# Splitting the down projection's first operand and weights under the second half of the last up product, with the halves of that product swapped

## The chip, the core and the metric

The kernel runs on one NeuronCore of a Trainium2 chip. The metric is the device time of one execution in microseconds. Three executions of the kernel before took 1459.34, 1459.81 and 1460.95 us; the median is 1459.81.

## What is computed

One inference step of a decoder layer with 1024 prompt tokens and 64 sample tokens (8 sequences of 8), width 1024, inner width 2816, all in 32-bit floats. The layer has a mixing part (stick-breaking attention and a convolution branch) and a channel part; the change touches only the channel part:

```
h2 = x * (1 + sc2) + sh2
val, gt = split(h2 @ w_up)                 # w_up: 1024 x 5632
gt_c = causal_dwconv(gt, width 3)          # per channel, along the tokens
f = (gelu(gt_c) * val) @ w_down            # w_down: 2816 x 1024
x = layernorm(alpha * x + (1 + g2) * f)
```

## The kernel before, in words

**Numbers.** Every matmul operand is split into a high and a low part of TensorE's 32-bit format: `split` (lines 594 to 596) makes the high part with a copy on ScalarE and the low part with a subtraction on VectorE. A product is then three matmuls: high by high, high by low, low by high.

**The up projection.** The 2816 inner channels are 22 feature tiles of 128. For each, `up_weights(f)` loads two 512 KB rows of `w_up` into two buffers of the ring `raw` (three buffers of 4 KB per partition) and makes seven 512-wide combinations of them, split into `W[0]` to `W[6]`. `up(f, ...)` multiplies them with the seven prepared combinations of the tokens: a fast matrix multiplication with seven half-size products in place of eight. The tokens come in two groups g of 272 columns for each product: `X[0]` lies in the pool `h2x`, `X[1]` (called Y in the profile, allocated at line 1571) in the six slots of ring "kv" in pool `kvp` and the two slots of ring "wo" in pool `wop`. A group's seven products of 12 matmuls go into three PSUM banks, and after each product `evacuate` (lines 1728 to 1742) reads its bank: products 0 and 3 on ScalarE, the others on VectorE. Product 3 may start when product 0 has been read, 4 after 1, 5 after 2 and 6 after 4. Feature tiles 1 to 20 take both groups together; the last one, 21, takes group 0 (X) and then group 1 (Y), line 1842.

**The gate.** `gate(f)` (lines 1812 to 1834) runs the width-3 convolution on VectorE (lines 1824 to 1828), gelu on ScalarE (1829) and the multiplication with the values on GpSimd (1831), and stores the result to DRAM scratch `fscr` and `fsscr` from SP's queue (1832, 1833).

**The down projection.** Three groups of feature tiles (8, 7 and 7) are accumulated over nine token tiles. For each token tile `f_tile` loads the gated features (line 1919) and splits them into `ft`; `prefetch` loads rows of `w_down` (line 626, called from 1908), 512 KB each, through `raw`, and splits them into a ring of 12 buffers `wd` of 8 KB. A token tile of the first group takes 8 x 6 = 48 matmuls of 512 columns (line 1942) into a pair of PSUM banks, which is copied to `acc` (line 1957). The weights of all later feature tiles reuse the 12 slots in turn.

**Where buffers lie.** The pools on the left side of the memory are stacked: `kvp`, `wop`, `arn` (with `W[4]`, `W[5]` and a sum), `h2x`, `gpp`. They are closed after the last gate (line 1848) and the pool `wdp` of the down projection (ring "ft" of two slots, "wd" of twelve, "fr" of two) is opened over the same bytes, so `ft` and the first weights lie where Y was. The first feature load is the exception: it goes to a `raw` buffer (line 1917). A wait is set for each buffer and each earlier reader of its bytes.

**What sets the order.** The stages up to the first up product are ordered by a planner inside the kernel. From there on (lines 1836 and following) the order of instructions on each engine and on SP's DMA queue is set at build time by the framework, which simulates the program's time line and lets instructions of the same engine pass each other where the data allows; on the chip every engine then keeps that fixed order.

Of the kernel before, what the change touches and what calls it, by code (L numbers as in the profile page):

```python
# [7 lines left out]
F32 = mybir.dt.float32  # L8
F32R = mybir.dt.float32r
# [7 lines left out]
D = 1024  # L17
TP = 1024
TS = 64
T = TP + TS  # L20
KT = 8
NFF = 22
# [10 lines left out]
NW = 12  # L33
KVB = 6
# [28 lines left out]
GROUPS = ((0, 8), (8, 15), (15, NFF))  # L63
# [409 lines left out]
def body(nc, tc, d):  # L473
    V, A, G, PE, SY = nc.vector, nc.scalar, nc.gpsimd, nc.tensor, nc.sync
# [14 lines left out]
    per = Open(name="per")  # L489
    rawp = Open(name="rawp")  # L490
    drp = Open(name="drp", space=DRAM)
    catp = Open(name="catp", side="right")
# [7 lines left out]
    def raw(shape, dt=F32):  # L500
        return rawp.tile(shape, dt, "raw", bufs=3)
# [7 lines left out]
    def vc(n, i=0, j=None, k=1):  # L509
        a = VEC[n][0] + i  # L510
        return vec[:, a:a + (k if j is None else j - i)]
# [19 lines left out]
    fscr = drp.tile([128, 4, NFF, 256], F32, "fscr")  # L531
    fsscr = drp.tile([128, NFF, TS], F32, "fsscr")
# [61 lines left out]
    def split(x, hi, lo):  # L594
        A.activation(hi, x, AF.Copy)  # L595
        V.tensor_sub(lo, x, hi)  # L596
# [22 lines left out]
        split(r, h, l)  # L619
        return h, l  # L620

    def split_pair(src, pool, name, bufs, r=None):

        if r is None:
            r = raw([128, D])
        SY.dma_start(r, src)
        w = pool.tile([128, 2, D], F32R, name, bufs=bufs)
        split(r, w[:, 0], w[:, 1])
        return w

# [312 lines left out]
    psS = Open(name="psS", space=PSUM)  # L943
    scr = [psS.tile([128, 2, 256], F32, f"scr{i}") for i in range(2)]
    psB = Open(name="psB", space=PSUM)
    kvp = Open(name="kvp")
# [296 lines left out]
    wop = []  # L1243
# [159 lines left out]
    wop, arn = wop  # L1403
# [4 lines left out]
    h2x = Open(name="h2x")  # L1408
    gpp = Open(name="gpp")
    vtp = Open(name="vtp", side="right")  # L1410
    cp = Open(name="cp", side="right")
    psC = Open(name="psC", space=PSUM)
# [4 lines left out]
    def bank():  # L1417
        npu[0] += 1
        return pus[(npu[0] - 1) % 8]
# [373 lines left out]
    dp = Open(name="dp", side="right")  # L1793
# [5 lines left out]
    def up(f, gss, vt, gp, gs):  # L1799
        for gg in gss:  # L1800
            P = [{g: bank() for g in gg} for _ in range(3)]
            for i in range(7):
                p = P[SUMS[i]]
                for kt in range(4):
                    for wt, xt, n in ((0, 0, 0), (0, 1, 1), (1, 0, 2)):
                        for g in gg:
                            PE.matmul(p[g][:, 0:NB], W[i][wt][:, 128 * kt:128 * kt + 128], X[g][kt][xt][:, i, :],  # L1807
                                      start=i < 3 and kt == 0 and n == 0, stop=kt == 3 and n == 2, skip_group_check=True)
                for g in gg:
                    evacuate(i, p[g], g, vt, gp, gs)  # L1810

    def gate(f, vt, gp, gs):
        V.memset(gp[:, 0:2], 0.0)
        V.tensor_copy(gs[:, :, 0:2], sft[:, f])
        V.tensor_copy(fop[:, f], gp[:, TP:TP + 2])
        V.tensor_copy(fos[:, f], gs[:, :, 8:10])
        c = dp.tile([128, 4, NB], F32, "gc", bufs=2)
        cp_, cs_ = c[:, :, 0:256], c[:, :, 256:NB].rearrange("p a (b t) -> p a b t", t=8)
        for k in range(3):
            w = vc("w_fdw", f * 3 + k)  # L1820
            gpk = gp[:, k:k + TP].rearrange("p (a i) -> p a i", a=4)
            gsk = gs[:, :, k:k + 8].rearrange("p (a b) t -> p a b t", a=4)
            if k == 0:
                V.tensor_scalar(cp_, gpk, w, vc("b_fdw", f), op0=OP.mult, op1=OP.add)
                V.tensor_scalar(cs_, gsk, w, vc("b_fdw", f), op0=OP.mult, op1=OP.add)
            else:
                V.scalar_tensor_tensor(cp_, gpk, w, cp_, op0=OP.mult, op1=OP.add)
                V.scalar_tensor_tensor(cs_, gsk, w, cs_, op0=OP.mult, op1=OP.add)
        gelu = A.activation(c, c, AF.Gelu).ins
        v4 = vt.rearrange("p h g i -> p (h g) i")  # L1830
        G.tensor_tensor(v4, v4, c, op=OP.mult)
        SY.dma_start(fscr[:, :, f, :], v4[:, :, 0:256])
        SY.dma_start(fsscr[:, f].rearrange("p (a i) -> p a i", a=4), v4[:, :, 256:NB])
        return gelu

    gate(0, vtb(), gp0(), gs0)
    for f in range(1, NFF):
        if f > 1:
            up_weights(f)
        t = (dp.tile([128, 2, 2, NB], F32, "vt", bufs=2), dp.tile([128, 2 + TP], F32, "gp", bufs=2),  # L1840
             dp.tile([128, 8, 10], F32, "gs", bufs=2))
        up(f, ((0,), (1,)) if f == NFF - 1 else ((0, 1),), *t)
        gelu = gate(f, *t)
    G.dma_start(d["ffn_p"], fop)
    G.dma_start(d["ffn_s"], fos)
    with tc.issue_after(gelu):
        pre[0] = A.preload_act_table_set(NLE).ins
    for p in (gpp, h2x, arn, wop, kvp, psC, psS, dp, vtp, catp):
        p.close()


    wdp = Open(name="wdp")
    ep = Open(name="ep", side="right")
    psE = Open(name="psE", space=PSUM)
    acc = [ep.tile([128, D], F32, f"acc{i}") for i in range(9)]
# [2 lines left out]
    def load_rows(i):  # L1858
        rows[i] = ep.tile([128, 2, D], F32, "rows", bufs=1)
        SY.dma_start(rows[i], d["lnr"][2 * i:2 * i + 2].unsqueeze(0).to_broadcast([128, 2, D]))  # L1860
        if i == 0:
            A.activation(rows[0], rows[0], AF.Copy, scale=ALPHA)
# [38 lines left out]
            V.scalar_tensor_tensor(y[0:n, h], y[0:n, h], r, rows[1][0:n, 1, h], op0=OP.mult, op1=OP.add)  # L1901
            SY.dma_start(d["y"][t0:t0 + n, h], y[0:n, h])

    ws = []

    def prefetch(n):
        for f in range(len(ws), min(n, NFF)):
            ws.append(split_pair(d["w_down"][f], wdp, "wd", NW))

    def f_tile(grp, tt):  # L1910
        f0, f1 = GROUPS[grp]
        nf, n = f1 - f0, min(128, T - 128 * tt)
        if grp or tt:
            fr = wdp.tile([128, 8, 128], F32, "fr", bufs=2)[:, 0:nf, 0:n]
        else:

            fr = raw([128, 1024]).rearrange("p (f n) -> p f n", n=128)
        fx = wdp.tile([128, 2, 8, 128], F32R, "ft", bufs=2)
        SY.dma_start(fr, fscr[:, tt // 2, f0:f1, 128 * (tt % 2):128 * (tt % 2) + n] if tt < 8 else fsscr[:, f0:f1])
        if tt < 8:  # L1920
            split(fr, fx[:, 0, 0:nf], fx[:, 1, 0:nf])
            return fx, ((0, 0), (0, 1), (1, 0))
        split(fr, fx[:, 0, 0:nf, 0:TS], fx[:, 0, 0:nf, TS:128])
        return fx, ((0, 0), (0, 1))

    for grp, (f0, f1) in enumerate(GROUPS):
        nf = f1 - f0
        for tt in range(9) if grp < 2 else (8, *range(8)):
            t0 = 128 * tt
            n = min(128, T - t0)  # L1930
            fx, passes = f_tile(grp, tt)
            prefetch(f1)
            last = (grp, tt) == (2, 7)
            pd = [psE.tile([128, 2, 512], F32, "pd", bufs=4) for _ in range(4 if last else 1)]
            pd = [p[:, 0, 0:256] for p in pd] if last else [pd[0][:, c] for c in range(2)]
            cw = D // len(pd)
            for cs_ in [(c,) for c in range(4)] if last else [(0, 1)]:
                for i in range(nf):
                    w = ws[f0 + i]
                    for xt, wt in passes:  # L1940
                        for c in cs_:
                            PE.matmul(pd[c], fx[:, xt, i], w[:, wt, cw * c:cw * c + cw],  # L1942
                                      start=i == 0 and (xt, wt) == passes[0], stop=i == nf - 1 and (xt, wt) == passes[-1])
            prefetch(min(len(ws) + 1, f0 + NW))
            if (grp, tt) == (0, 2):
                load_rows(0)
                load_gates()
            if (grp, tt) == (1, 8):
                load_rows(1)
            a, g = acc[tt], g2.get("p" if tt < 8 else "s")  # L1950
            if grp == 2:
                finish(tt, pd, t0, n, g)
                continue
            for c in range(2):
                h = slice(512 * c, 512 * c + 512)
                if grp == 0:
                    V.tensor_copy(a[:, h], pd[c])
                else:
                    V.tensor_add(a[:, h], a[:, h], pd[c])
            if grp == 1:  # L1960
                x = ep.tile([128, D], F32, "fx", bufs=2)
                SY.dma_start(x[0:n], xscr[t0:t0 + n, :])
                G.tensor_tensor(x[0:n], x[0:n], rows[0][0:n, 0], op=OP.mult)  # L1963
                G.tensor_tensor(x[0:n], x[0:n], rows[0][0:n, 1], op=OP.add)
                V.tensor_mul(a, a, g)
                V.tensor_add(a[0:n], a[0:n], x[0:n])
    for p in (psE, ep, wdp, drp, rawp, per):
        p.close()


# [80 lines left out]
```

## Time and profile before

| | us |
|---|---|
| median of the three runs | 1459.81 |
| the profiled execution | 1459.86 |
| its span, from the first to the last instruction | 1458.1 |
| TensorE (matmuls) busy | 1406.1 |
| VectorE busy | 1069.2 |
| ScalarE busy | 618.4 |
| GpSimd busy | 579.8 |

Read it as a chain that runs almost wholly on TensorE; the mean granted clock of TensorE over the span is 0.984 of 2.4 GHz. Positions in the text are microseconds from the start of the span. The last feature tile's up product runs from about 1160 to 1182, the down projection from there to about 1449. In the profile PE is TensorE, PEld its weight loads, DVE VectorE, ACT ScalarE, POOL GpSimd, SPq SP's queue of DMA issues. In a line of a timeline the bracket gives the engine's idle time just before it and what ended it; several like instructions are merged into one line with their count.

### The profile page before, as it was taken

The page shows a single profiled execution, that of the slowest core. Times are in us where ns is not written, and L with a number is a line of the kernel's source. Part 1 is how long each engine was busy: PE and PEld are TensorE (multiplying, and loading weights), DVE is VectorE, ACT ScalarE, POOL GpSimd, SP SyncE. Part 2 cuts the span into 40 slices and gives each one's busy share as a digit, 9 for nine tenths or more (in the row PEclk, how much of TensorE's full clock was granted, in tenths as well). Part 3 has the DMA queues.
Part 4 walks back from the last instruction along what each step waited for, and adds up shares of the span by engine and source line. Part 5 has one row for each costly group of instructions (what it writes and reads, how often), then busy time and mean ns, then how long its engine had stood idle before and what let it go on. Part 6 is the DMA issues. An engine that isn't in the chain of part 4 may idle for free.

```text
span 1458.1 us, 26948 instructions
## 1 busy us (share of the span) xinstructions
PE 1406.1 (96%) x10254; PEld 1224.0 (84%) x10254; DVE 1069.2 (73%) x1903; ACT 618.4 (42%) x1236; POOL 579.8 (40%) x433
## 2 busy tenths in 40 slices
PE   7999999998999999799899999999999989999997
PEld 4898899985666666588799999999999978888886
DVE  4799997536677666587978877787777754168798
ACT  2454524638888888233543332333333332031110
POOL 0398833226464534422534443443344213016300
PEclk9999999999999999899899999999999999999999
DMA  8855533257988787533122222222222266152331
GB/s 324 284 162 186 152 121 106 100 191 239 322 292 314 273 288 257 158 117 123 58 93 75 90 74 75 75 85 78 75 75 74 89 195 216 33 179 83 108 102 72
DMA packets 116987, 219.26 MB, mean 150 GB/s; under 512 B 28673, under 2 KB 71210, under 8 KB 116602
## 3 DMA queue, kind: packets, MB, share of 16 engines
q1 hardware_dynamic: 113498, 206.03, 43.1%
q0 software_dynamic: 3360, 11.51, 2.2%
q8 instruction: 81, 1.33, 0.4%
q14 instruction: 48, 0.39, 0.1%
HBM read 184.31 MB, written 32.68 MB: 149 GB/s over the span
## 4 chain that ended last, share of the span: by engine, by line
PE 66%; DVE 4%; issue 1%; ACT 1%; POOL 0%; DVEq 0%; ACTq 0%; POOLq 0%
PE pu L1807 23%; PE pd L1942 18%; PE scr L1807 7%; PE pu L1506 3%; PE scr L1506 2%; PE acc L1127 2%; PE z L1117 2%; PE scr L1260 1%; PE acc L1316 1%; PE z L1071 1%; PE z L1072 1%; PE pu L1746 1%; PE scr L1746 1%; PE scr L1299 1%; PE scr L1300 1%
## 5 line engine op out<-in xcount | busy, mean ns | idle before, releaser
L1942 PE MATMUL pd<-wd,ft 128*128 128x512 f32 (+1 forms) x1186 | 263.6, 385 | 4.0 <-DVE wd L596 1.5
L1942 PEld LDWEIGHTS pd<-wd,ft 128*128 128x128 f32 x1186 | 218.9, 190 | 48.7 <-DVE wd L596 1.9
L1807 PE MATMUL pu<-X,wA 128*128 128x272 f32 x768 | 187.7, 288 | 0.0
L1807 PE MATMUL pu<-Y,wA 128*128 128x272 f32 x756 | 186.8, 288 | 0.0
L636 PE MATMUL po<-HH,whi 128*128 128x378 f32 (+1 forms) x464 | 152.4, 337 | 0.5 <-ACT HH L595 0.5
L636 PE MATMUL po<-HL,whi 128*128 128x378 f32 (+1 forms) x464 | 151.4, 332 | 0.4 <-DVE HL L596 0.4
L636 PE MATMUL po<-HH,wlo 128*128 128x378 f32 (+1 forms) x464 | 150.7, 331 | 0.0
L1113 POOL TENSOR_TENSOR ll<-l,lh 127x512 fp32r<-127x512 f32 (+4 forms) x92 | 96.5, 1050 | 113.7 <-DVE lh L1110 82.9
L1807 PEld LDWEIGHTS pu<-X,wA 128*128 128x128 f32 x768 | 141.5, 188 | 0.0
L1807 PEld LDWEIGHTS pu<-Y,wA 128*128 128x128 f32 x756 | 140.5, 189 | 0.0
L872 ACT ACTIVATE l<-z 127x512 f32<-127x512 f32 (+11 forms) x272 | 119.9, 476 | 33.3 <-PE z L1117 12.7
L724 DVE SCALAR_TENSOR_TENSOR pc<-u,vec,pc 128x1024 f32<-128x1024 f32 x80 | 102.8, 1285 | 1.8
L636 PEld LDWEIGHTS po<-HH,whi 128*128 128x128 f32 x464 | 86.5, 188 | 11.2 <-issue 8.3
L1783 POOL TENSOR_TENSOR cc__8834<-raw 128x512 f32<-128x512 f32 x20 | 31.3, 1566 | 157.9 <-DMA raw<-w_up 157.9
L596 DVE TENSOR_TENSOR wA<-raw,wA 128x512 fp32r<-128x512 f32 x60 | 74.5, 1243 | 22.7 <-ACT wA L595 22.6
L636 PEld LDWEIGHTS po<-HL,whi 128*128 128x128 f32 x464 | 86.5, 188 | 4.4 <-issue 1.3
L708 POOL TENSOR_TENSOR cv<-cv,q 128x1024 f32<-128x1024 f32 x36 | 88.4, 2455 | 2.8 <-ACT q L707 1.1
L1082 DVE SCALAR_TENSOR_TENSOR l<-l,z 127x512 f32<-127x512 f32 (+4 forms) x96 | 53.4, 557 | 48.8 <-ACT l L872 47.4
L636 PEld LDWEIGHTS po<-HH,wlo 128*128 128x128 f32 x464 | 86.9, 188 | 1.8 <-issue 1.3
L595 ACT ACTIVATE wA<-raw 128x512 fp32r<-128x512 f32 x60 | 38.0, 635 | 113.8 <-PE pu L1807 61.5
L595 ACT ACTIVATE ft<-fr 128x896 fp32r<-128x896 f32 (+3 forms) x26 | 24.4, 939 | 121.2 <-PE pd L1942 121.1
L1963 POOL TENSOR_TENSOR fx<-fx,rows 128x1024 f32<-128x1024 f32 (+1 forms) x9 | 24.6, 2742 | 122.8 <-DVE ft L596 76.0
(654 smaller groups left out, 3598.8 us busy)
## 6 DMA issues: line engine op xcount, KB each, us to landing
kv<-kv SPq DMA_DIRECT2D x128, 512.0 KB
catt<-w_ada SPq DMA_DIRECT2D x48, 512.0 KB
raw<-w_up SPq DMA_DIRECT2D x44, 512.0 KB
fscr<-vt SPq DMA_DIRECT2D x22, 512.0 KB
raw<-w_down SPq DMA_DIRECT2D x22, 512.0 KB
raw<-w_in SPq DMA_DIRECT2D x20, 512.0 KB
fr<-fscr SPq DMA_DIRECT2D x16, 448.0 KB
xT<-xT SPq DMA_DIRECT2D x8, 544.0 KB
```

Of the source, the lines that this page charges most:

```text
L595: A.activation(hi, x, AF.Copy)
L596: V.tensor_sub(lo, x, hi)
L636: PE.matmul(ps[c][:, 0:b - a], wt[:, 128 * kt:128 * kt + 128], xt[:, kt, a:b], start=first and kt == 0, stop=last and kt == KT - 1)
L708: G.tensor_tensor(op, op, t[:, 0:TP], op=OP.add)
L724: V.scalar_tensor_tensor(pcs[c], src, w, pcs[c], op0=OP.mult, op1=OP.add)
L872: A.activation(out, in_, f, **kw)
L1082: V.scalar_tensor_tensor(out, e, ZMAX, z, op0=OP.min, op1=OP.max)
L1113: (V if eng == "DVE" else G).tensor_tensor(t.hl[1], t.l, t.hl[0], op=OP.subtract)
L1506: PE.matmul(po[c](), xs()[:, xt, kt % 4], WO[kt][:, wt, 512 * c:512 * c + 512], start=kt == KORD[0] and (xt, wt) == passes[0], stop=kt == ...
L1783: G.tensor_tensor(s1, a21, a22, op=OP.add)
L1807: PE.matmul(p[g][:, 0:NB], W[i][wt][:, 128 * kt:128 * kt + 128], X[g][kt][xt][:, i, :], start=i < 3 and kt == 0 and n == 0, stop=kt == 3 a ...
L1942: PE.matmul(pd[c], fx[:, xt, i], w[:, wt, cw * c:cw * c + cw], start=i == 0 and (xt, wt) == passes[0], stop=i == nf - 1 and (xt, wt) == pa ...
```

## The change

In the last feature tile the two token groups are swapped: group 1 (Y) first, then group 0 (X). Between them stand the first call of `f_tile` and `prefetch(2)`, behind them `prefetch(5)`. The pool `kvp` stays open: its ring of six "kv" slots, where six of Y's eight buffers lay, now takes the first split features `ft` and weights 0 to 4. The weights are kept in two rings of six slots, "kv" in `kvp` and "wd" in `wdp`, in turn: weights 5 to 10 go to "wd", 11 to 16 to "kv", 17 to 21 to "wd". Weights 2, 3 and 4 are loaded not into `raw` but into two 8 KB buffers "wr" in the ring "wo" of `wop`, where Y's last two buffers lay. `wdp` now starts above `kvp`, over `wop`, `arn` and `h2x`. `split_pair` is given its target instead of a pool. Everything else, the arithmetic and the number of instructions among it, is as before.

```diff
-    def split_pair(src, pool, name, bufs, r=None):
+    def split_pair(src, w, r=None):
...
         SY.dma_start(r, src)
-        w = pool.tile([128, 2, D], F32R, name, bufs=bufs)
         split(r, w[:, 0], w[:, 1])
         return w
...
+    ws, wdp, early = [], [], []
+
+    def prefetch(n):
+        for f in range(len(ws), min(n, NFF)):
+            n = (f + 1) // KVB % 2
+            w = wdp[0].tile([128, 2, D], F32R, "wd", bufs=NW - KVB) if n else kvp.tile([128, 2, D], F32R, "wd", bufs=KVB, tag="kv")
+            if 2 <= f < KVB - 1:
+
+                if f % 2 == 0:
+                    early.append(wop.tile([128, 2, D], F32, "wr", bufs=KT - KVB, tag="wo"))
+                ws.append(split_pair(d["w_down"][f], w, early[-1][:, f % 2]))
+            else:
+                ws.append(split_pair(d["w_down"][f], w))
+
+    def f_tile(grp, tt):
+        f0, f1 = GROUPS[grp]
+        nf, n = f1 - f0, min(128, T - 128 * tt)
+        if grp or tt:
+            fr = wdp[0].tile([128, 8, 128], F32, "fr", bufs=2)[:, 0:nf, 0:n]
+            fx = wdp[0].tile([128, 2, 8, 128], F32R, "ft", bufs=2)
+        else:
+            fr = raw([128, 1024]).rearrange("p (f n) -> p f n", n=128)
+            fx = kvp.tile([128, 2 * D], F32R, "ft", bufs=KVB, tag="kv").rearrange("p (x f n) -> p x f n", x=2, n=128)
...
-        up(f, ((0,), (1,)) if f == NFF - 1 else ((0, 1),), *t)
+        if f == NFF - 1:
+
+            up(f, ((1,),), *t)
+            ahead = f_tile(0, 0)
+            prefetch(2)
+            up(f, ((0,),), *t)
+            prefetch(KVB - 1)
+        else:
+            up(f, ((0, 1),), *t)
         gelu = gate(f, *t)
...
-    for p in (gpp, h2x, arn, wop, kvp, psC, psS, dp, vtp, catp):
+    for p in (gpp, h2x, arn, wop, psC, psS, dp, vtp, catp):
         p.close()
...
-    wdp = Open(name="wdp")
+    wdp.append(Open(name="wdp"))
...
-            fx, passes = f_tile(grp, tt)
+            fx, passes = f_tile(grp, tt) if grp or tt else ahead
             prefetch(f1)
...
-    for p in (psE, ep, wdp, drp, rawp, per):
+    for p in (psE, ep, wdp[0], kvp, drp, rawp, per):
         p.close()
```

## Rows read from the trace of the kernel before

**Rows 1.** The page: the busy time of each engine (share of the span, instructions), and the group row of the down projection's matmuls (count, busy us, mean ns, idle us just before them and the releaser of most of it).

```profile
PE 1406.1 (96%) x10254; PEld 1224.0 (84%) x10254; DVE 1069.2 (73%) x1903; ACT 618.4 (42%) x1236; POOL 579.8 (40%) x433
...
L1942 PE MATMUL pd<-wd,ft 128*128 128x512 f32 (+1 forms) x1186 | 263.6, 385 | 4.0 <-DVE wd L596 1.5
```

**Rows 2.** The timeline of TensorE's matmuls around the seam of the two projections: start, us, engine, line, instruction and count, and in the bracket the idle time before it with its releaser.

```profile
1170.82 1.67 PE L1807 MATMUL pu<-Y,wA 128*128 128x272 f32 x12
1172.33 1.66 PE L1807 MATMUL pu<-X,w 128*128 128x272 f32 x12
...
1180.23 1.68 PE L1807 MATMUL pu<-Y,w 128*128 128x272 f32 x12
1183.25 0.73 PE L1942 MATMUL pd<-wd,ft 128*128 128x512 f32 x2 [1.34 <-ACT wd L595]
1185.14 0.73 PE L1942 MATMUL pd<-wd,ft 128*128 128x512 f32 x2 [1.16 <-ACT ft L595]
1187.33 12.95 PE L1942 MATMUL pd<-wd,ft 128*128 128x512 f32 x43 [1.46 <-DVE wd L596]
```

**Rows 3.** The timeline of VectorE and ScalarE at the same place: the evacuation of the sixth (L1740) and seventh product (L1742), the last gate's steps (L1824 to L1828), and splits (L595 on ScalarE, L596 on VectorE).

```profile
1180.43 0.42 DVE L1740 TENSOR_TENSOR gp<-gp,scr 128x256 f32<-128x256 f32 x1 [1.08 <-PE scr L1807]
...
1180.96 0.81 DVE L1824 TENSOR_SCALAR gc<-gp,vec 128x1024 f32<-128x1024 f32 x1
1181.18 1.07 ACT L595 ACTIVATE ft<-raw 128x1024 fp32r<-128x1024 f32 x1 [3.32 <-PE pu L1807]
...
1181.76 0.31 DVE L1825 TENSOR_SCALAR gc<-gs,vec 128x64 f32<-128x64 f32 x1
1181.98 0.43 DVE L1742 TENSOR_TENSOR vt<-vt,pu 128x272 f32<-128x272 f32 x1
...
1182.33 1.28 DVE L1827 SCALAR_TENSOR_TENSOR gc<-gp,vec,gc 128x1024 f32<-128x1024 f32 x1
...
1183.52 0.28 DVE L1828 SCALAR_TENSOR_TENSOR gc<-gs,vec,gc 128x64 f32<-128x64 f32 x1
1183.72 1.22 DVE L596 TENSOR_TENSOR ft<-raw,ft 128x1024 fp32r<-128x1024 f32 x1
...
1193.66 1.07 ACT L595 ACTIVATE wd<-raw 128x1024 fp32r<-128x1024 f32 x1 [0.28 <-DMA raw<-w_down]
```

**Rows 4.** Stretches of one microsecond: length, then busy time of each engine (with instructions), TensorE's granted clock, the DMA share and GB/s.

```profile
1186.00:1187.00 1.00, 0.00 (x0) 0.00 (x0) 1.00 (x2) 0.00 (x0) 0.00 (x0) 0.84 0.70 184
1187.00:1188.00 1.00, 0.67 (x2) 0.58 (x3) 1.00 (x3) 0.44 (x1) 0.00 (x0) 0.50 0.80 324
...
1193.00:1194.00 1.00, 1.00 (x5) 0.76 (x4) 0.78 (x2) 0.72 (x2) 0.00 (x0) 0.75 1.13 348
```

**Rows 5.** The timeline of VectorE: copies of finished token tiles out of PSUM (two for each tile) for the first tile and from the fourth on.

```profile
1207.11 1.29 DVE L1957 COPY acc<-pd 128x512 f32<-128x512 f32 x2 [2.77 <-PE pd L1942]
...
1233.18 1.29 DVE L1957 COPY acc<-pd 128x512 f32<-128x512 f32 x2 [6.12 <-PE pd L1942]
...
1244.13 1.29 DVE L1957 COPY acc<-pd 128x512 f32<-128x512 f32 x2 [8.53 <-PE pd L1942]
...
1255.01 1.29 DVE L1957 COPY acc<-pd 128x512 f32<-128x512 f32 x2 [8.46 <-PE pd L1942]
```

**Rows 6.** The timeline of SP's queue: DMA issues (L626 weights of the down projection, L1919 features, L1832 the gate's store); several issues are merged into one line, whose time is from the first to the last.

```profile
1159.31 4.13 SPq L626 DMA_DIRECT2D raw<-w_down  x2
...
1173.53 1.00 SPq L1919 DMA_DIRECT2D fr<-fscr  x2
1184.97 3.99 SPq L626 DMA_DIRECT2D raw<-w_down  x3
...
1192.13 0.52 SPq L1832 DMA_DIRECT2D fscr<-vt  x1
```

**Rows 7.** The timeline of VectorE during the second half of feature tile 21.

```profile
1174.03 0.44 DVE L1742 TENSOR_TENSOR vt<-vt,pu 128x272 f32<-128x272 f32 x1 [2.50 <-PE pu L1807]
1174.48 0.42 DVE L1732 TENSOR_TENSOR gp<-vt,pu 128x256 f32<-128x256 f32 x1
1174.82 0.16 DVE L1732 TENSOR_TENSOR gs<-vt,pu 128x16 f32<-128x16 f32 x1
...
1178.91 0.44 DVE L1738 TENSOR_TENSOR vt<-vt,pu 128x272 f32<-128x272 f32 x1 [2.55 <-PE pu L1807]
```

**Rows 8.** Stretches of one microsecond while the first weight's load runs alone; the last two columns are the DMA share and GB/s.

```profile
1160.00:1161.00 1.00, 1.00 (x10) 1.00 (x10) 1.00 (x4) 0.31 (x1) 0.00 (x0) 1.00 0.28 66
1161.00:1162.00 1.00, 1.00 (x10) 1.00 (x9) 1.00 (x3) 0.33 (x1) 0.00 (x0) 1.00 0.90 340
```

**Rows 9.** Stretches of an earlier stage (length, TensorE busy, ..., granted clock): one of four microseconds in which TensorE is about half idle, and two around the end of a longer gap.

```profile
584.00:588.00 4.00, 2.23 (x37) 1.29 (x36) 4.00 (x5) 1.97 (x5) 2.75 (x1) 1.00 0.05 18
...
710.00:711.00 1.00, 0.00 (x0) 0.00 (x0) 1.00 (x3) 0.69 (x2) 0.92 (x2) 1.00 0.15 57
...
712.00:713.00 1.00, 1.00 (x6) 1.00 (x6) 1.00 (x2) 0.33 (x1) 0.92 (x2) 0.61 0.00 0
```

**Rows 10.** The timeline: the gate's multiply on GpSimd for feature tiles 20 and 21, and a split on VectorE beside the second.

```profile
1165.68 2.53 POOL L1831 TENSOR_TENSOR vt<-vt,gc 128x1088 f32<-128x1088 f32 x1 [11.21 <-ACT gc L1829]
...
1188.81 3.29 POOL L1831 TENSOR_TENSOR vt<-vt,gc 128x1088 f32<-128x1088 f32 x1 [6.06 <-ACT gc L1829]
...
1191.08 2.11 DVE L596 TENSOR_TENSOR wd<-raw,wd 128x1024 fp32r<-128x1024 f32 x1 [1.34 <-ACT wd L595]
```

More of the change, by code (lines that the diff above doesn't have):

```diff
@@ L1834, in gate @@
         return gelu
+    ws, wdp, early = [], [], []
[18 more added lines that the diff above has]
+            fx = kvp.tile([128, 2 * D], F32R, "ft", bufs=KVB, tag="kv").rearrange("p (x f n) -> p x f n", x=2, n=128)
+        SY.dma_start(fr, fscr[:, tt // 2, f0:f1, 128 * (tt % 2):128 * (tt % 2) + n] if tt < 8 else fsscr[:, f0:f1])
+        if tt < 8:
+            split(fr, fx[:, 0, 0:nf], fx[:, 1, 0:nf])
+            return fx, ((0, 0), (0, 1), (1, 0))
+        split(fr, fx[:, 0, 0:nf, 0:TS], fx[:, 0, 0:nf, TS:128])
+        return fx, ((0, 0), (0, 1))
     gate(0, vtb(), gp0(), gs0)
@@ L1902, in finish @@
             SY.dma_start(d["y"][t0:t0 + n, h], y[0:n, h])
[L1904 to L1924, printed above, removed]
     for grp, (f0, f1) in enumerate(GROUPS):
```

## The prediction

> **What bounds the kernel now.** The page comes first: TensorE is busy 96% of the span, so a change can win only where TensorE is idle or slow. The group row of the down projection (L1942) says where: all its 1186 matmuls had 4.0 us of idle time ahead of them [rows 1]. The timeline puts it at the seam between the up projection (L1807) and the down projection: the last twelve up matmuls start at 1180.23, two down matmuls run at 1183.25, two at 1185.14, and the steady stream starts at 1187.33. The brackets name three different releasers: ScalarE on a weight, ScalarE on the operand, VectorE on a weight [rows 2]. The timelines of these two engines show why: the first operand's split starts only at 1181.18, having waited 3.32 us for the up matmuls that still read the buffers over which it is written. Then every split (1.07 us on ScalarE, 1.22 us on VectorE) stands in the open, mixed on VectorE with the last gate [rows 3]. Last, the one-microsecond windows: after these gaps the granted clock falls to 0.50 (1.2 GHz) in 1186 to 1187 and is back at 1.00 (2.4 GHz) from about 1193.5 [rows 4].
>
> **What the seam costs.** Twelve up matmuls issue in 1.51 us (groups of 12 start at 1170.82 and 1172.33 [rows 2]), so TensorE could take the next one at 1180.23 + 1.51 = 1181.74. At the other end, the copies of finished token tiles start at 1207.11 (the first), 1233.18 (the fourth), 1244.13 and 1255.01 [rows 5]: a tile of 48 matmuls takes 10.88 us, 0.227 for one and 1.36 for one feature tile's six. Four tiles without loss would have begun at 1233.18 - 4 x 10.88 = 1189.66, less 0.24 us from a last issue to its reader (1181.98 - 1181.74, [rows 2, 3]): 1189.4. The seam costs 1189.4 - 1181.7 = **7.7 us**. Check by parts: 4.0 us idle, two pairs that each end 0.28 us later than in a stream (0.73 against 2 x 0.227), and 6.2 us at half rate, which is 3.1: together 7.7. This is the most that the change can win; behind 1233 the tiles are evenly spaced and offer nothing.
>
> **The swap of the halves** moves no matmul in or out: 84 for either half. The order on each engine is the build's planner's: in the trace it put 12 matmuls of the second half (Y) ahead of the first half's last product [rows 2]. I take the mirrored order: the half that reads Y ends where X's ended, its last product starting at 1172.33. The operand's split followed the start of that product by 0.95 us (1181.18 - 1180.23), so it now starts at about 1173.3, not 1181.2. TensorE loses nothing if the evacuations of the second half stay on time (below).
>
> **Operand and weights 0 and 1.** Their loads are moved past nothing that holds them: the raw buffers are the same three, and the two weight loads left SP in the group from 1159.31 on [rows 6]; the features' load was earlier still. ScalarE: three times 1.07 from 1173.3, done at 1176.5. VectorE: three times 1.22 beside evacuations of 0.16 to 0.44; in that stretch it had holes of up to 2.5 us between them [rows 7], so done by about 1178. That is over 3 us ahead of 1181.7. Cost: nothing, hidden under the second half's ten microseconds of matmuls.
>
> **Weights 2, 3, 4** are staged in the two slots of Y's last buffers, free at about 1174.3. Their three SP issues wait there. Behind them on SP are the loads of 5 to 7, which wait for raw buffers, and the features of the next two tiles, which wait for X: issued at 1173.53 before, now at about 1181.6. A lone load has most of its bytes moved about 2.7 us after issue (1159.31; 340 GB/s in 1161 to 1162) [rows 6, 8], and 512 KB at that rate is 1.5 us for each further one. With 3.3 us for the first they land at 1177.6, 1179.1 and 1180.7, and are split by 1182 to 1184. TensorE wants weight 2 at 1181.7 + 2 x 1.36 = 1184.4 and weight 4 at 1187.2. Cost: nothing. Were they as slow as the three loads at the old seam, issued from 1184.97 on and the last one waited for until 1193.66 [rows 3, 6], so 8.7 us, weight 4 would land at 1183.0 and be split at 1185.3, still in time.
>
> **Weights 5, 6, 7** are the tight ones. They lie over the staging of 2 to 4 and over the small buffers beside it, so their splits follow those. VectorE must do, from 1174.4 on, eight weights and the operand (nine splits, 11.0), the second half's evacuations (four of 0.44, two of 0.42 and two of 0.16: 2.9) and the last gate (0.81 + 0.31 + 2 x 1.28 + 2 x 0.28 and two short copies, 4.6) [rows 3, 7]. That is 18.5 us without a hole: 1192.9. TensorE wants the low part of weight 7 at 1181.7 + 7 x 1.36 + 0.45 = 1191.7. So the stall lies between 0 (splits ahead of the gate) and 1.2 us (gate first); I take **0.6**, as the planner at the old seam put the operand's split between two steps of the gate [rows 3].
>
> **The seam itself.** The first PSUM tile of the down projection may lie where the second half's sixth product is read out. That reading started at 1180.43 [rows 3]; a split put ahead of it costs up to 1.2 us. I take **0.3**: TensorE gets there at 1181.7 only, so most of a split is covered. The clock stays at 1.00 if idle time is this short: in 584 to 588 TensorE was busy 2.23 of 4 us and kept it [rows 9].
>
> **Later.** Ring reuse keeps its distance of 12: weight 11 takes the operand's slot, 12 that of weight 0, needed only in the second group, over eight tiles of 10.88 us later. The loads of rows and gates behind the weights on SP have the same distance. GpSimd's queue is moved past nothing. The tail is unchanged. Cost 0.
>
> **Sum.** -7.7 + 0.6 + 0.3 = -6.8, and 0.2 for small waits: -6.6 us. The profiled execution took 1459.86 (span 1458.1 and 1.8 around it), 0.05 above the median of the runs, 1459.81. Forecast: **1453.2**. Bounds of the likeliest case: all 7.7 won, 1452.1, to a loss of 1.2 at both places, 1454.6. A run can tell about 0.2% (2.9 us): faster means below 1456.9, slower above 1462.7.
>
> **Rival 1: VectorE and GpSimd get into each other's way under weights 6 and 7.** When the gate's multiply ran on GpSimd from 1188.81, a VectorE split that started at 1191.08 took 2.11 us, to 1.1 us behind the multiply's end; undisturbed it takes 1.22, and the multiply 2.53 [rows 3, 10]. In the changed kernel the gate ends on VectorE at about 1188, so gelu and the multiply come at 1189 to 1192, just when the last splits must be done. If the multiply gets in between, weight 7 is late by up to 2.5 us more. Then the saving is 7.7 - 0.9 - 2.5 = 4.3: **1455.5**. For it: the timing. Against: ScalarE's gelu comes first, and meanwhile a split fits. Chance 0.18. The Trainium skill, "SBUF — State Buffer" (SBUF: two separate sides), makes it an exclusive lock held for a whole instruction, the loser fully blocked; by that the full 2.5 us and this rival's time follow whenever the multiply starts first. The split's end just behind the multiply's agrees.
>
> **Rival 2: the wait comes back behind weight 4, long enough for the clock.** If the loads of 5 to 7 come into SP's queue behind the gate's store (1192.13 [rows 6]), they land at 1196 and later. TensorE has five weights and, with the second operand, ten blocks of 1.36: to 1195.3. A stall of 2 us and 3.1 us from the slow clock leave 7.7 - 5.1 = 2.6: **1457.2**. Against: the queue takes its issues as they come free (the features at 1173.53 went ahead of the weights of 1184.97 [rows 6]), and the raw buffers are free by 1178. Chance 0.09.
>
> **Rival 3: slower.** VectorE keeps its order. If weight 4's split is put ahead of the evacuation of the second half's fifth product, for which the seventh waits, TensorE stops in the up projection until that load has landed. With landing at L, the split (1.07 + 1.22), the evacuation (0.44) and 0.2 between them, the seventh product starts at L + 2.9, not at 1180.2. At L = 1180.7 that is 3.4 us and, as after the gap of some 3 us ahead of 712 [rows 9], the slow clock, 3.1: saving 1.2. From L = 1184.8 on (10.6 us lost) it is slower by more than can be mistaken; at 1186, 8.7 + 3.1 - 7.7 = 4.1 slower: **1463.9**. Against it is the speed of loads [rows 8]. Chance 0.08.
>
> **Rival 4: nothing moves**, because a ring slot is not released before X too: 1459.8. Against: features for the next tiles were loaded over X at 1173.53 while Y was still being read [rows 2, 6], so release goes by buffer. Chance 0.05.
>
> **The numbers.** 0.60 for the forecast's case, 1452.1 to 1454.6. Half a microsecond of noise below and the whole of rival 1 above give 1451.6 to 1456.9, which leaves out rivals 3 and 4, most of 2 and little else: 0.2. Faster: 0.60 + 0.18 + 0.04 of rivals 2 and 3 = 0.82; slower, the worse part of rival 3: 0.07; the rest, 0.11, the same.
>
> **What would show it.** Right: the operand's split near 1173; no down matmul that waits more than 1 us; clock 1.00 through 1180 to 1200; the fourth tile's copy at about 1226.6; weights 5 to 7 as the last releasers, if any. Wrong: a clock of 0.50 behind the seam, an up product that waits for VectorE between 1174 and 1182, or SP issuing weight 5 after 1190.

## The result, and the profile after

| | before | after |
|---|---|---|
| median of the runs compared, us | 1459.57 (4 runs, 1458.24 to 1460.95) | 1451.47 (4 runs, 1450.12 to 1451.63) |
| ratio, with its 95% interval | | 0.9947 [0.9936, 0.9959] |
| profiled execution, us (its span) | 1459.86 (1458.1) | 1451.63 (1449.9) |
| first product of feature tile 21 starts at | 1160.68 | 1159.82 |
| last matmul ends at | 1449.48 | 1441.24 |
| between these two | 288.80 | 281.42 |

The change is faster: 8.1 us between the medians, 6.0 to 9.3 by the interval; 1453.2 had been forecast. The median stands 0.1 below the low end of the range, 1451.6; the ratio applied to 1459.81 gives 1452.1.

Not all of the 8.2 us between the two profiled executions is the change's. Ahead of tile 21 the order of instructions is the same on every engine, yet the execution after came there 0.86 us earlier. In the other kernels below, none of which is altered ahead of that place, it came at 1157.3 to 1160.2: this is what executions differ by. So the timelines of TensorE are compared from there on, and give 288.80 - 281.42 = **7.4 us**. All of it is won by the time of the fourth token tile's copy: 1233.18 - 1160.68 = 72.50 before [rows 5], 1224.94 - 1159.82 = 65.12 after, 7.38 less. Of the 7.7 that the seam cost, 0.3 is left.

The page after: busy time of the engines, and the group row of the down projection's matmuls (count, busy us, mean ns, idle us ahead of them).

```profile
PE 1402.1 (97%) x10254; PEld 1223.0 (84%) x10254; DVE 1064.7 (73%) x1903; ACT 617.2 (43%) x1236; POOL 579.6 (40%) x433
...
L1958 PE MATMUL pd<-wd,ft 128*128 128x512 f32 (+1 forms) x1186 | 260.1, 382 | 0.0
```

The instructions are as many as before, and the idle time of 4.0 us [rows 1] is 0.0. The timeline of TensorE's matmuls after, which answers to [rows 2]:

```profile
1171.47 1.67 PE L1806 MATMUL pu<-Y,w 128*128 128x272 f32 x12
...
1177.86 1.65 PE L1806 MATMUL scr<-X,cb__8878 128*128 128x272 f32 x12
1179.48 1.77 PE L1806 MATMUL pu<-X,w 128*128 128x272 f32 x12
1181.12 79.14 PE L1958 MATMUL pd<-wd,ft 128*128 128x512 f32 x348
```

No line has a bracket: 348 matmuls follow the up projection in one piece, in place of two pairs and a stream that started 7.1 us behind the last twelve up matmuls. The timeline of VectorE and ScalarE after, answering to [rows 3, 5, 7]:

```profile
1171.92 1.06 ACT L595 ACTIVATE ft<-raw 128x1024 fp32r<-128x1024 f32 x1 [0.97 <-PE pu L1806]
...
1176.76 1.06 ACT L595 ACTIVATE wd<-wr 128x1024 fp32r<-128x1024 f32 x1 [1.88 <-DMA wr<-w_down]
...
1178.99 0.43 DVE L1737 TENSOR_TENSOR vt<-vt,pu 128x272 f32<-128x272 f32 x1
1179.34 1.22 DVE L596 TENSOR_TENSOR wd<-wr,wd 128x1024 fp32r<-128x1024 f32 x1
1180.48 0.42 DVE L1739 TENSOR_TENSOR gp<-gp,scr 128x256 f32<-128x256 f32 x1
1180.81 0.17 DVE L1739 TENSOR_TENSOR gs<-gs,scr 128x16 f32<-128x16 f32 x1
...
1184.79 2.35 DVE L596 TENSOR_TENSOR wd<-raw,wd 128x1024 fp32r<-128x1024 f32 x2
...
1188.45 1.21 DVE L596 TENSOR_TENSOR wd<-raw,wd 128x1024 fp32r<-128x1024 f32 x1
...
1224.94 1.29 DVE L1973 COPY acc<-pd 128x512 f32<-128x512 f32 x2 [8.46 <-PE pd L1958]
```

The operand's split starts at 1171.92 in place of 1181.18; splits of weights now stand between the evacuations of the second half (L1737 reads the fifth product, the two lines of L1739 the sixth), where VectorE had holes of 2.50 and 2.55 us [rows 7]. The last line is the fourth tile's copy. SP's queue after, for [rows 6]:

```profile
1173.05 1.28 SPq L626 DMA_DIRECT2D wr<-w_down  x3
1174.42 3.55 SPq L626 DMA_DIRECT2D raw<-w_down  x3
1180.53 1.00 SPq L1859 DMA_DIRECT2D fr<-fscr  x2
```

Six weights are now issued ahead of the next tiles' features. One stretch of one microsecond while the last staged load is still under way, and the one in which the clock fell before (0.84 there, 0.50 behind it [rows 4]) (length, busy time and count of PE, PEld, DVE, ACT and POOL, granted clock, DMA share, GB/s):

```profile
1178.00:1179.00 1.00, 1.00 (x11) 1.00 (x10) 1.00 (x2) 1.00 (x3) 0.00 (x0) 1.00 1.04 426
...
1186.00:1187.00 1.00, 1.00 (x6) 0.84 (x5) 1.00 (x2) 0.53 (x1) 0.00 (x0) 1.00 0.34 113
```

TensorE is busy without a break and its clock stays at 1.00 (2.4 GHz), in these two stretches and in every other microsecond from 1178 to 1203.

### The profile page after: what moved, and what is told of

It reads as the page before. It is cut to its first block, busy times and chain, and to the rows that moved or that the text cites. A ratio compares the mean times of both kernels' runs of the same rounds, so it can differ in the third digit from the quotient of the medians.

```text
span 1449.9 us, 26940 instructions
## 1 busy us (share of the span) xinstructions
PE 1402.1 (97%) x10254; PEld 1223.0 (84%) x10254; DVE 1064.7 (73%) x1903; ACT 617.2 (43%) x1236; POOL 579.6 (40%) x433
## 4 chain that ended last, share of the span: by engine, by line
PE 66%; DVE 3%; ACT 1%; issue 1%; POOL 0%; DVEq 0%; ACTq 0%; POOLq 0%
PE pu L1806 23%; PE pd L1958 18%; PE scr L1806 7%; PE pu L1505 4%; PE scr L1505 2%; PE acc L1126 2%; PE z L1116 2%; PE scr L1259 1%; PE acc L1315 1%; PE z L1070 1%; PE z L1071 1%; PE pu L1745 1%; PE scr L1745 1%; PE scr L1298 1%; PE scr L1299 1%
## 5 line engine op out<-in xcount | busy, mean ns | idle before, releaser
L1958 PE MATMUL pd<-wd,ft 128*128 128x512 f32 (+1 forms) x1186 | 260.1, 382 | 0.0
L1782 POOL TENSOR_TENSOR cc__8834<-raw 128x512 f32<-128x512 f32 x20 | 34.9, 1744 | 158.3 <-DMA raw<-w_up 158.3
L596 DVE TENSOR_TENSOR wA<-raw,wA 128x512 fp32r<-128x512 f32 x60 | 74.5, 1243 | 23.0 <-ACT wA L595 23.0
L595 ACT ACTIVATE wA<-raw 128x512 fp32r<-128x512 f32 x60 | 37.9, 633 | 116.9 <-PE pu L1806 61.5
L595 ACT ACTIVATE ft<-fr 128x896 fp32r<-128x896 f32 (+3 forms) x26 | 24.4, 939 | 129.2 <-PE pd L1958 127.2
L1830 POOL TENSOR_TENSOR vt<-vt,gc 128x1088 f32<-128x1088 f32 x22 | 57.7, 2623 | 29.2 <-ACT gc L1828 29.2
```

## The experiments

For each kernel the length from tile 21's first product to the last matmul is given, read as in the table above; it is free of the differences ahead of the seam. Before: 288.80, after: 281.42, and 281.1 if nothing were lost. How late a group starts is reckoned from the start of the one ahead, with 0.227 us for each of its down matmuls; the idle time in a bracket is a little shorter, since a group's last matmul still runs out.

### The swap alone (e1_swap_only)

The kernel before with the two halves swapped, pools and loads left as they were.

```diff
-        up(f, ((0,), (1,)) if f == NFF - 1 else ((0, 1),), *t)
+        up(f, ((1,), (0,)) if f == NFF - 1 else ((0, 1),), *t)
```

> The kernel before with the two halves of the last up product swapped and nothing else: the pool of Y is still closed behind the last gate, one ring of twelve weights, no staging. Theory A (what counts is when Y's bytes are free): the operand's split moves to about 1172, the gap at the seam goes, 1451.5 to 1453. Theory B (a split can enter the engines' fixed order only behind the place where the new pool is opened, so the open ring is needed): VectorE still does the last gate's first steps before the operand's low part, which stays near 1184; TensorE still waits and its clock still falls; 0 to 2 us saved, 1457.5 to 1459.6.

Measured: 1461.02 against 1459.75, ratio 1.0011 [1.0003, 1.002]; length 289.65. The swap by itself wins nothing: theory B's mechanism, with a time 1.4 us above its range. The timeline of this kernel at the seam:

```profile
1177.21 1.06 ACT L595 ACTIVATE ft<-raw 128x1024 fp32r<-128x1024 f32 x1
...
1180.83 1.01 SPq L1919 DMA_DIRECT2D fr<-fscr  x2
1181.14 0.64 PE L1942 MATMUL pd<-wd,ft 128*128 128x512 f32 x2
...
1183.15 1.22 DVE L596 TENSOR_TENSOR ft<-raw,ft 128x1024 fp32r<-128x1024 f32 x1
...
1185.06 1.06 ACT L595 ACTIVATE ft<-fr 128x1024 fp32r<-128x1024 f32 x1 [3.04 <-DMA fr<-fscr]
1186.17 23.31 PE L1942 MATMUL pd<-wd,ft 128*128 128x512 f32 x94 [4.39 <-ACT ft L595]
```

ScalarE does split the operand early, and the first pair of matmuls follows the up projection without a gap. But VectorE keeps its fixed order and makes the low part behind two steps of the gate (1183.15), and the features of the next tile, which lie over X, are issued at 1180.83 in place of 1173.53 [rows 6]. The build had put that tile's matmuls next, so TensorE waits 4.39 us for its operand. One long wait has taken the place of three; behind it the clock is at 0.50 until about 1189.9, and at 1210.83 and 1212.28 TensorE waits for operands again, 1.35 and 0.26 us.

### Rings and staging without the swap (e2_no_swap)

The changed kernel with X first and Y second, and the calls behind both.

```diff
-            up(f, ((1,),), *t)
+            up(f, ((0,), (1,)), *t)
             ahead = f_tile(0, 0)
-            prefetch(2)
-            up(f, ((0,),), *t)
             prefetch(KVB - 1)
```

> The changed kernel without the swap: X first, then Y, then the first operand and weights 0 to 4 in the open ring, ahead of the gate in the program. Theory A and B alike: Y's buffers come free only at the end of the up product, so the operand's split stays near 1181, the clock falls, and what is saved is only the gate's steps between the splits: 0 to 2 us, 1457.5 to 1459.6. Rival (the splits' place ahead of the gate is what won): 1453 to 1455.

Measured: 1457.83 against 1459.75, ratio 0.9991 [0.9982, 1.0]; length 287.79, so 1.0 saved in the traces; by the times alone the two kernels can hardly be told apart. Its timeline:

```profile
1178.05 1.06 ACT L595 ACTIVATE ft<-raw 128x1024 fp32r<-128x1024 f32 x1 [2.81 <-PE pu L1806]
...
1180.11 0.73 PE L1956 MATMUL pd<-wd,ft 128*128 128x512 f32 x2 [0.83 <-ACT wd L595]
1183.50 8.71 PE L1956 MATMUL pd<-wd,ft 128*128 128x512 f32 x30 [2.67 <-DVE wd L596]
1192.93 57.42 PE L1956 MATMUL pd<-wd,ft 128*128 128x512 f32 x252 [0.71 <-DVE wd L596]
```

Ring "kv" is not free before Y has been read, so the operand's split again waits for the last up matmuls, and 4.2 us of idle time stand in the open. The two halves of the change are worth -0.9 and 1.0 us apart and 7.4 together: the swap frees the buffers, the open ring lets the splits use them.

### Where the calls stand in the program (e8_behind_both)

The changed kernel with both halves in one call and the loads and splits written behind them.

```diff
-            up(f, ((1,),), *t)
+            up(f, ((1,), (0,)), *t)
             ahead = f_tile(0, 0)
-            prefetch(2)
-            up(f, ((0,),), *t)
             prefetch(KVB - 1)
```

> The changed kernel with the first operand and weights 0 and 1 called behind both halves in the program, not between them; ring, staging and swapped halves as changed. If the planner hoists them because the ring's slots are free (theory B's reading), the order and the time are those of the changed kernel: 1451 to 1452. If their place between the halves is needed: splits behind the second half's last evacuation, 1455 or more.

Measured: 1450.88 against 1459.75, ratio 0.9942 [0.9929, 0.9955]; length 281.35. The built program has the same instructions in the same order as the changed kernel on every engine, so this is also a repetition of it: the length came out within 0.1 us. TensorE's timeline again has one piece without a bracket:

```profile
1180.45 69.87 PE L1956 MATMUL pd<-wd,ft 128*128 128x512 f32 x307
```

The build moves the splits forward by itself where the slots are free, and the calls between the halves do nothing. In the swap alone it left VectorE's order nearly as it was; there the splits go into a pool that is opened behind the gate, over closed ones. That this is the reason is argued from the code and was not tried apart.

### The staging of weights 2 to 4 (e3_no_staging)

The changed kernel with these weights loaded through the three raw buffers like the others.

```diff
-            if 2 <= f < KVB - 1:
+            if False:
```

> The changed kernel with weights 2, 3 and 4 loaded through the three raw buffers like the others, not into the staging over Y's last buffers. Theory (the early place of the splits is what counts, and a raw buffer comes free in time): weight 2 is loaded when the operand's low part is done at 1174.2, 3 and 4 after weights 0 and 1, each some 3.3 us from issue to landing, against needs of 1183.8, 1185.2 and 1186.6; weights 5 to 7 follow by 1187 to 1190 and are wanted from 1187.9 on: 0 to 1 us lost, 1451 to 1452.5. Rival (the staging is needed): a wait behind weight 4 and the slow clock, 1454 to 1457.

Measured: 1456.26 against 1458.99, ratio 0.9978 [0.9969, 0.9987]; length 285.31, 3.9 more than after. I had expected next to nothing; the rival held. SP's queue and TensorE in its timeline:

```profile
1171.79 6.17 SPq L626 DMA_DIRECT2D raw<-w_down  x4
1178.01 1.62 SPq L1859 DMA_DIRECT2D fr<-fscr  x2
...
1178.36 6.08 PE L1958 MATMUL pd<-wd,ft 128*128 128x512 f32 x26
...
1180.25 6.49 SPq L626 DMA_DIRECT2D raw<-w_down  x3
...
1186.96 68.37 PE L1958 MATMUL pd<-wd,ft 128*128 128x512 f32 x294 [2.52 <-ACT ft L595]
```

With three buffers for everything, four loads take 6.17 us to be issued (three staged ones took 1.28), since each waits for a split to free its buffer. The build has put the next token tile's matmuls behind the first 26, and their operand is late: its features, issued at 1178.01 ahead of weights 6 and 7, land at 1185.8. TensorE starts again 2.70 us late (1186.96 for 1178.36 + 26 x 0.227), and the clock falls, as the stretches show:

```profile
1186.00:1187.00 1.00, 0.04 (x1) 0.04 (x1) 1.00 (x2) 0.91 (x1) 0.00 (x0) 0.81 1.02 393
1187.00:1188.00 1.00, 1.00 (x3) 0.81 (x4) 1.00 (x3) 0.02 (x1) 0.00 (x0) 0.50 1.06 359
...
1189.00:1190.00 1.00, 1.00 (x4) 0.81 (x3) 0.93 (x1) 0.85 (x2) 0.00 (x0) 0.50 0.45 182
```

From 1186.96 to 1190 it runs at half rate, which costs 1.5. With 2.70 that makes 4.2, and 4.2 is what this length has above 281.1.

### How much room weights 5 to 7 have (e5_low_twice)

The low parts of these three weights are computed twice, 1.14 us of VectorE's time each.

```diff
         split(r, w[:, 0], w[:, 1])
+        for _ in range(again):
+            V.tensor_sub(w[:, 1], r, w[:, 0])
...
-                ws.append(split_pair(d["w_down"][f], w))
+                ws.append(split_pair(d["w_down"][f], w, None, 1 if 5 <= f < 8 else 0))
```

> The changed kernel with the low parts of weights 5, 6 and 7 computed twice, 3.7 us more on VectorE at the seam. In the changed kernel these parts are ready 2.4, 2.6 and 1.4 us ahead of TensorE's need. If that is all the slack there is, TensorE waits 2 to 6 us (the repeats stand behind splits of the next operands and beside the gate's multiply on GpSimd) and loses 0 to 3 more to the clock: 1454 to 1461. Rival (VectorE is nowhere near a limit and the planner finds room): below 1452.5.

Measured: 1452.45 against 1458.99, ratio 0.9957 [0.9941, 0.9972]; length 282.03, 0.6 more than after. I had expected 1454 or more; the rival held. Of 3.4 us of added work TensorE saw one wait of 0.37, less than the room of 1.4 us would have let through. The reason is the order: the build put eight matmuls of the next two token tiles ahead of weight 5's low part. TensorE would have wanted that at 1180.57 + 32 x 0.227 = 1187.8, with the eight at 1189.65, and got it at 1190.31, 0.66 late: the 0.6 of the length. So the run doesn't measure the room by itself; it shows that the order fills what is missing. Its timeline also shows what the extra work did to GpSimd:

```profile
1189.03 1.22 DVE L629 TENSOR_TENSOR wd<-raw,wd 128x1024 fp32r<-128x1024 f32 x1
1189.82 7.37 POOL L1832 TENSOR_TENSOR vt<-vt,gc 128x1088 f32<-128x1088 f32 x1 [6.62 <-ACT gc L1830]
...
1190.31 59.91 PE L1960 MATMUL pd<-wd,ft 128*128 128x512 f32 x263 [0.37 <-DVE wd L629]
...
1193.58 1.22 DVE L629 TENSOR_TENSOR wd<-raw,wd 128x1024 fp32r<-128x1024 f32 x1
1195.09 3.18 DVE L596 TENSOR_TENSOR wd<-raw,wd 128x1024 fp32r<-128x1024 f32 x1 [0.30 <-ACT wd L595]
```

The gate's multiply, 2.53 us undisturbed [rows 10], took 7.37. VectorE's instructions followed each other without a hole until 1194.80; the multiply ended at 1197.19, 2.4 us behind that, and the next split 1.08 us later.

### How much room the evacuations have (e7_early_twice)

The same repetition for weights 2 to 4, whose splits stand among the evacuations of the second half.

```diff
-                ws.append(split_pair(d["w_down"][f], w, early[-1][:, f % 2]))
+                ws.append(split_pair(d["w_down"][f], w, early[-1][:, f % 2], 1))
```

> The changed kernel with the low parts of weights 2, 3 and 4 computed twice, 3.7 us more on VectorE while the second half's products are being read out. VectorE works in order: the reading of the sixth product, in whose bank the down projection's first tile is summed, is put back by 1.1 us behind a repeat, so TensorE waits about 1.0 us at the seam, then 1 to 2 us for weights 5 to 7: 1452.5 to 1454.5. If the seam does not hang on VectorE's order: no wait at the seam, 1451.5. If the mechanism of the prediction's slower rival bites (TensorE stopped in the up product, then slow clock): 1456 or more.

Measured: 1452.95 against 1458.99, ratio 0.9956 [0.9941, 0.9972]; length 282.93, 1.5 more than after. The timeline:

```profile
1180.53 1.22 DVE L629 TENSOR_TENSOR wd<-wr,wd 128x1024 fp32r<-128x1024 f32 x1
1181.66 0.41 DVE L1741 TENSOR_TENSOR gp<-gp,scr 128x256 f32<-128x256 f32 x1
...
1182.30 67.95 PE L1960 MATMUL pd<-wd,ft 128*128 128x512 f32 x297 [0.99 <-DVE gs L1741]
...
1190.98 0.76 PEld L1960 LDWEIGHTS pd<-wd,ft 128*128 128x128 f32 x4 [0.21 <-ACT ft L595]
1192.05 2.14 PEld L1960 LDWEIGHTS pd<-wd,ft 128*128 128x128 f32 x10 [0.31 <-DVE wd L596]
1194.44 11.64 PEld L1960 LDWEIGHTS pd<-wd,ft 128*128 128x128 f32 x52 [0.26 <-ACT ft L595]
```

One repeated subtraction pushes the sixth product's evacuation back by its own length, and TensorE, which writes its first down product into that bank, starts it 1.13 us later than after. So this evacuation has no room: what VectorE puts ahead of it beyond the changed kernel's splits shows at once. The other 0.4 us was lost from 1190.8 to 1194.8, where TensorE's weight loads (PEld) waited 0.21, 0.31 and 0.26 us for parts of the next operands and of a weight; I had put down 1 to 2 us there.

### GpSimd beside VectorE (e6_gpsimd_block)

Two additions on GpSimd that read weight 4's parts, behind the last prefetch; their result is not used.

```diff
             prefetch(KVB - 1)
+            z = dp.tile([128, D], F32, "z")
+            for _ in range(2):
+                G.tensor_tensor(z, ws[4][:, 1], ws[4][:, 0], op=OP.add)
```

> The changed kernel with two needless additions on GpSimd that read weight 4's two parts (2.5 us each, into a scratch tile), from about 1182 to 1187, beside the last gate and the splits of weights 5 and 6 on VectorE. If GpSimd and VectorE exclude each other for whole instructions, VectorE falls up to 5 us behind and the low parts of weights 5 to 7 come up to 3.6 us late; with the slow clock 1455 to 1458. If they share without loss: 1451.5 and VectorE's durations unchanged.

Measured: 1454.96 against 1458.99, ratio 0.9972 [0.996, 0.9984]; length 284.84, 3.4 more than after. Its timeline:

```profile
1182.53 2.90 POOL L1881 TENSOR_TENSOR z<-wd 128x1024 f32<-128x1024 f32 x1 [10.45 <-DVE wd L596]
1183.07 2.38 DVE L1815 COPY fos<-gs 128x16 f32<-128x16 f32 x1
...
1185.94 3.90 DVE L1826 SCALAR_TENSOR_TENSOR gc<-gp,vec,gc 128x1024 f32<-128x1024 f32 x1
1186.33 2.41 POOL L1881 TENSOR_TENSOR z<-wd 128x1024 f32<-128x1024 f32 x1
...
1191.22 3.06 PE L1961 MATMUL pd<-wd,ft 128*128 128x512 f32 x12 [2.27 <-DVE wd L596]
1194.88 55.38 PE L1961 MATMUL pd<-wd,ft 128*128 128x512 f32 x243 [0.61 <-DVE wd L596]
```

A copy of 16 columns, 0.17 us in the changed kernel, took 2.38, and a gate step of 1.28 took 3.90: the copy ended with GpSimd's first addition (1185.45 and 1185.43), the gate step 1.10 us behind the second (1189.84 and 1188.74). The weights came late, and so did TensorE: 2.52 us (1191.22 for 1181.44 + 32 x 0.227) and 0.94 (1194.88 for 1191.22 + 12 x 0.227), together the 3.4 that were lost. The clock was granted at 1.00 in every microsecond from 1190 to 1196 and took nothing.

### Holding the clock up at the old seam (e4_clock_fill)

The kernel before with 44 matmuls of 272 columns behind the last up product, into a bank whose content is no longer needed.

```diff
+        if f == NFF - 1:
+            p = pus[(npu[0] - 1) % 8]
+            for i in range(44):
+                PE.matmul(p[:, 0:NB], W[6][0][:, 0:128], X[0][3][1][:, 6, :], start=i == 0, stop=i == 43, skip_group_check=True)
```

> The kernel before with 44 needless matmuls of 272 columns (5.5 us) behind the last up product, into a PSUM bank already read out; their sums are not used. They fill the idle time at the seam. The planner then puts all of the last gate ahead of the operand's low part, so the down projection's stream should begin at about 1188.1 and not 1187.33, 0.8 later. If the 3.1 us of half clock come from the idle time, the clock stays at 1.00 and 2.3 us are won all the same: 1457.3. If the clock falls for another reason (the change of the kind of matmul), it falls here too: 1460.4.

Measured: 1472.32 against 1459.75, ratio 1.0083 [1.007, 1.0096]; length 303.92. A miss for both readings: 12.6 us slower. The fillers took 5.73 us at clock 1.00, but the build answered them with another order. ScalarE did gelu and a table load first and split the operand only at 1186.23; TensorE stood idle behind the fillers after all and again some 30 us later:

```profile
1188.29 0.91 PE L1946 MATMUL pd<-wd,ft 128*128 128x512 f32 x2 [2.30 <-ACT wd L595]
1189.82 24.25 PE L1946 MATMUL pd<-wd,ft 128*128 128x512 f32 x94 [0.62 <-DVE wd L596]
...
1219.15 3.60 PE L1946 MATMUL pd<-wd,ft 128*128 128x512 f32 x8 [5.08 <-ACT ft L595]
1224.91 25.27 PE L1946 MATMUL pd<-wd,ft 128*128 128x512 f32 x103 [2.17 <-DVE ft L596]
```

It says nothing on the clock's share at the old seam. That share, 3.1 of the 7.7, stays worked out from the granted clock and not measured apart; what supports it are two sums, e3_no_staging with a half rate that is needed to make up the loss, and e6_gpsimd_block without one and without need of one.

## Why the prediction was right, step by step

**What the seam costs: right.** 7.7 was the bound, 7.4 was won in the traces. What is left: the last up product starts 0.11 us late, the first down matmul 0.13 us behind its earliest time (1181.12 against 1179.48 + 1.51), and the fourth copy 0.06 behind 1181.12 + 4 x 10.88 + 0.24. The fourth copy had been forecast at 1226.6; set against the same start it came at 1224.94 + 0.86 = 1225.8. None of the other kernels has a length more than 0.1 below the changed one's (e8_behind_both, the same order), and at this place none could by more than 0.3. By its own terms the likeliest case ends at 1452.1 + 2.4 = 1454.5, not 1454.6.

**The swap, the operand, weights 0 and 1: right.** Of the 1.4 us by which the split came earlier than put down (1171.92 for 1173.3), 0.86 are the whole execution's; it followed the start of the first half's last product (1171.47) by 0.45 instead of 0.95.

**Weights 2 to 4: right.** They were issued together at 1173.05, the first had landed by 1176.76 and the third by 1179.2, where I had 1177.6 and 1180.7: less 0.86, the first is on time and the third 0.6 early. Several loads at once, the staged ones and from 1174.42 on those of weights 5 to 7 beside them, moved 401 to 426 GB/s in each microsecond from 1175 to 1179; my 340 was the rate of a load running alone. That the staging costs nothing was right; what it is worth, 3.9 us in the traces and so half of the gain, only e3_no_staging showed, and I had not expected it.

**Weights 5 to 7: the term of 0.6 was mis-sized; it is 0.** The work is the one that I listed, 18.5 us, but it was done between 1173.01 and 1189.66, in 16.65. The durations in a timeline overlap: a split listed with 1.22 us is followed by the next instruction 1.14 behind its start (1179.34 to 1180.48). For the 24 instructions of this stretch that is 1.8; 18.5 less 1.8, less a short copy that had run at 1170.63 (0.17), plus one hole of 0.24 is 16.7. So weight 7 was complete at 1189.66, where TensorE wanted it at 1181.12 + 7 x 1.36 + 0.45 = 1191.1: 1.4 us of room. The build did put weights 5 and 6 between two steps of the gate.

**The seam itself: 0.3 forecast, 0.13 found**, by the mechanism forecast. A split (1179.34) stood ahead of the sixth product's evacuation. That came at 1180.48, 2.62 us behind its product's start (1177.86), where before it was 1.72 (1178.71 to 1180.43): 0.9 later. Most of this was covered, as put down: the evacuation's second part ended at 1180.81 + 0.17 = 1180.98, the first down matmul followed 0.14 behind it and was 0.13 late. e7_early_twice shows what one subtraction more ahead of it costs, 0.99.

**Small waits: 0.2 forecast, 0.17 found**, the 0.11 ahead of the last up product and the 0.06 at the copy. The sum of the three terms was 1.1 and should have been 0.3: forecast 6.6, traces 7.4. The rest of the 8.1 between the medians is inside its interval.

**Rival 1** is a real mechanism that found nothing to delay. In the changed kernel the multiply started on GpSimd at 1190.35, 0.7 us behind weight 7. Its price was right in kind: e6_gpsimd_block made VectorE late by 2.2 and 2.6 us per instruction and cost 3.4. The Trainium skill, "SBUF — State Buffer" (SBUF: two separate sides), has an exclusive lock that whoever starts first holds for the whole instruction. The runs agree that one engine stands still for whole instructions of the other, on both sides: 2.38 us for 0.17 and 7.37 for 2.53. By the listed starts they do not bear out who holds it: the gate step listed from 1185.94 ended behind an addition listed from 1186.33 (e6_gpsimd_block), and the multiply listed from 1189.82 behind splits listed up to 1193.58 (e5_low_twice). In e5_low_twice VectorE's splits, without a hole between them, kept GpSimd out for 5 us; in e6_gpsimd_block the first addition got in between two VectorE instructions (1182.35 and 1183.07) that had no hole between them either. What decides whether the multiply gets in between, on which this rival hangs, stays open.

**Rival 2** did not come: weights 5 to 7 left SP's queue from 1174.42 on, ahead of the features and 20 us ahead of the gate's store. Something like it came in e3_no_staging, where features and weights changed places in the queue.

**Rival 3**, slower, came in the small: the low part of a staged weight stood ahead of the fifth product's evacuation, which came at 1178.99 and held the seventh product up for 0.11 us. The third load had landed at 1179.2, 4.7 us ahead of the point from which this rival decides (1184.8, less 0.86 for the earlier start).

**Rival 4** did not come: the splits and loads went out while X was being read.

## What to carry to other kernels

To close a gap between two stages, see both that the buffers come free early and that the instructions that use them can move there: here either alone won 1 us or lost 0.9, both won 7.4. Count an engine's load by the distance between starts, not by the listed durations, and a load's time by what runs beside it. Staging buffers that let several loads be issued at once can be worth much: here half of what was won.

## What the runs showed of the hardware that I had not expected

- VectorE starts the next instruction 0.08 us before the listed end of the one ahead (1.22 listed, 1.14 between starts).
- GpSimd's multiply took 7.37 us in place of 2.53 while VectorE issued splits without a hole (e5_low_twice). It ended 2.39 us behind the end of the VectorE instruction ahead of the first hole, and so it did before (1192.10 and 1189.74), after (1194.34 and 1191.94) and in e7_early_twice (1196.68 and 1194.27): 2.36 to 2.41, about its own length. A VectorE copy of 16 columns took 2.38 in place of 0.17 beside a GpSimd addition (e6_gpsimd_block).
- TensorE's clock fell to 0.50 (1.2 GHz) behind waits of 2.52 us (e3_no_staging), 2.67 (e2_no_swap), 4.39 (e1_swap_only), 2.30 and, later, 5.08 and 2.17 (e4_clock_fill). It stayed at 1.00 behind waits of 2.27 and 0.61 (e6_gpsimd_block), of 0.99 (e7_early_twice) and of 1.35 (e1_swap_only, at 1210.83). The 2.17 that cost it and the 2.27 that did not show that the length of one wait alone does not decide; what does is open.
